# A two-layer hybrid block in split fp32: the opening's loads and root, the key weights' tiles, the conformer's input product, and the second mixer's order are changed

## The chip, the cores and the metric

The kernel runs on one core of one Trainium2 chip. The metric is the device time of one execution in microseconds (us); of the kernel before, three runs were timed. The profile is one further execution, recorded by the hardware profiler. TensorE (PE in the profile) multiplies, VectorE (DVE) and ScalarE (ACT) do elementwise work, GpSimd (POOL) little, and SyncE (SP) issues nearly all DMAs.

## The reference

The block has two layers on 256 tokens `x` and 256 context tokens, 1024 channels wide. Each layer is a half feed-forward, a mixer, and a second half feed-forward; the context goes through all of the first layer, and through the second only as far as the second mixer's keys, values and decays.

```python
x = half_ffn(x, sx[0], sx[1], sx[2], p['ffn1_norm'], p['ffn1_wi'], p['ffn1_wo'])   # and ctx
u_x = modulate(rms_norm(x, p['mix_norm']), sx[3], sx[4]) @ p['w_in']               # and ctx
x = x + sx[5] * mix_tokens(u_x, rows, dirs_x, states_x, p)
x = half_ffn(x, sx[6], sx[7], sx[8], p['ffn2_norm'], p['ffn2_wi'], p['ffn2_wo'])

def conformer_conv(u, dw_w, dw_b, ln_g, ln_b):
    a, g = jnp.split(u, 2, axis=-1)
    h = depthwise_conv(a * jax.nn.sigmoid(g), dw_w, dw_b)
```

`half_ffn` normalises (x times the inverse root of its mean square), scales and shifts by vectors that a product of a conditioning vector with the 1024 by 9216 matrix `ada_w` gives, and applies a gated feed-forward of width 2816. `mix_tokens` joins four mixers: a pooling mixer, a long convolution (hyena), a gated linear attention with decay in chunks of 64 tokens, forward and backward, and the conformer convolution above. All of it is fp32.

## The kernel before, in words

**Products.** Channels lie on partitions, tokens along the free dimension: the 512 tokens of x and context are eight tiles of 128 by 512. An fp32 product is three passes: each operand is split in a high part (a cast on ACT, L172) and a rest (a subtraction on DVE, L173), and `mm3` (L184 to L186) does high by high, high by rest, rest by high. Weights come as raw tiles of up to 1 MB (pool `raw`, 3 buffers) and are split into the pools `whi` and `wlo`, two buffers each; activations and intermediates of 128 by 512 share a pool of 28 buffers (`self.h`), and temporaries one of five. A tile takes a buffer in turn and waits until the last user of that buffer is done.

**Order.** Outside the opening, a planner at compile time sets the order on each engine from program order, priorities (`prio(-PRE)` pulls weight loads, splits and evictions ahead) and its own cost estimates. On the chip each engine takes its instructions in that order.

**Opening** (`start`, its PE, DVE and ACT work in hand-written order). x is loaded as eight tiles of 256 KB, alternating between SP's and ACT's DMA queues (L377); SP then issues the first 2 MB slab of `ada_w` (`ada_fetch`, slab 0), the small vectors and the identity, the first halves of two feed-forward weight tiles, slabs 1 and 2, the second halves, and slab 3. DMAs take eight completion semaphores in turn, and a DMA is issued only when the last user of its semaphore has landed. TensorE first does 48 warm-up products on ones (L152). ACT squares each x tile and DVE adds the squares (L383, L387); `rstd` takes the mean over partitions with 16 small products (L400, L401), and `rsqrt_cols` takes the inverse root on DVE by a shift and three Newton steps, column by column (L211 to L222). Then `part(0)` multiplies slab 0 by the conditioning vector (L287), `keep` does products on ones (L158), `spread` makes diagonal tiles of the root and broadcasts them with TensorE (L232, L234), `ada_end` transposes the row (L299), and DVE and ACT scale and shift x (L425, L432, L433). The products of two 128-row weight tiles follow (L1314 to L1317), interleaved with `part(1)` to `part(3)`.

**Feed-forwards.** 22 weight tiles up, then 8 output tiles down in two halves; between them DVE works off the rest of `ada_w` by multiply-add (L325), two pieces per weight tile.

**Mixer** (`mix`). For keys, values and decay inputs, queries and so on, `group` loads and splits the columns and `fm` (weights stationary) or `tm` (tokens stationary) multiplies. The keys' 128 columns go through `whi` and `wlo` like all others. `conv_in` (step C) loads the convolution's constants, then two groups of 256 columns, gate and value, and does two products of 256 columns for each 128 tokens, followed by tanh (L786) and a multiply (L787). `ORDERS` holds for each layer the program order of the steps: capitals and digits load and multiply a group (`0`, `1`, `2` are hyena's three, `R` gate, `P` pool, `Q` query), small letters advance a generator (`g` decay, states and readout, `h` hyena, `c` convolution, `p` pool, `G` output gate). `g`'s first step is the decay: ACT and DVE work on the product of L1079 up to the scan (L1094).

Of the kernel before, what the change touches and what calls it, by code (L numbers as in the profile page):

```python
# [9 lines left out]
F32 = mybir.dt.float32  # L10
F32R = mybir.dt.float32r
I32 = mybir.dt.int32
U8 = mybir.dt.uint8
AF = mybir.ActivationFunctionType
ALU = mybir.AluOpType
AX = mybir.AxisListType

P = 128
D = 1024
KT = D // P  # L20
# [6 lines left out]
C_K, C_V, C_G, C_Q, C_R, C_POOL, C_HY, C_CONV = 0, 128, 384, 416, 544, 800, 1056, 1824  # L27
# [7 lines left out]
PRE = 400  # L35
# [3 lines left out]
PZ = 2  # L39
F1 = (1.9, 0, 1)  # L40
F2 = (0.8, 0, 1.0, 20)
WARM = 48
KEEP = 2
PIECES = 2
ORDERS = ['Qgg0Rggg1hhghghgPgChcGhGchpchpGch2phpchch', 'Q0g1gggghCh2ghghghccRPhgGchphchchpphhcGpG']
ACTS = [(4, 5, 2, 3, 0, 1, 6, 7), (2, 3, 0, 1, 4, 5, 6, 7)]
TWO_PI_HI = 6.28125
TWO_PI_LO = 2.0 * math.pi - 6.28125
# [3 lines left out]
        ("hy_short_b", 6), ("pool_scale", 2), ("conv_ln_g", 2), ("conv_ln_b", 2), ("conv_dw_b", 2),  # L52
        ("gla_gb_f", 1), ("gla_gb_b", 1), ("gla_norm", 1)]
GROUPS = {"k": [(C_K, 128)], "q": [(C_Q, 128)], "vg": [(C_V, 256), (C_G, 32)], "hy0": [(C_HY, 256)], "hy1": [(C_HY + 256, 256)],
          "hy2": [(C_HY + 512, 256)], "cg": [(C_CONV + 256, 256)], "ca": [(C_CONV, 256)], "r": [(C_R, 256)], "pool": [(C_POOL, 256)]}


class Builder:
# [89 lines left out]
    def warm_up(self):  # L148

        ps = self.pa((P, P))  # L150
        for i in range(WARM):
            self.nc.tensor.matmul(ps, lhsT=self.ones, rhs=self.ones, start=True, stop=True)  # L152
# [35 lines left out]
    def rsqrt(self, src, n, scale):  # L188
        nc = self.nc
        v = self.small(n)  # L190
        nc.vector.tensor_scalar(v, src, scale, EPS, op0=ALU.mult, op1=ALU.add)
        i1 = self.small(n, I32)
        nc.vector.tensor_single_scalar(i1, v.bitcast(I32), 1, op=ALU.logical_shift_right)
        i2 = self.small(n, I32)
        nc.vector.tensor_scalar(i2, i1, -1.0, float(0x5F3759DF), op0=ALU.mult, op1=ALU.add)
        y = i2.bitcast(F32)
        for _ in range(3):
            a = self.small(n)
            nc.vector.scalar_tensor_tensor(a, y, -0.5, y, op0=ALU.mult, op1=ALU.mult)
            b = self.small(n)  # L200
            nc.vector.tensor_tensor(b, a, v, op=ALU.mult)
            y2 = self.small(n)
            nc.vector.scalar_tensor_tensor(y2, b, 1.5, y, op0=ALU.add, op1=ALU.mult)
            y = y2
        return y

# [167 lines left out]
    def load_x(self):  # L374
        self.x = [self.xp.tile([P, 512], F32, tag="x", name=self.nm("x")) for _ in range(KT)]
        for m in range(KT):
            (self.nc.scalar if m % 2 else self.nc.sync).dma_start(out=self.x[m], in_=self.t["xt"][m])  # L377

    def sumsq(self, m, lo, n):

# [8 lines left out]
        else:  # L389
            self.last_sq = sq  # L390

    def rstd(self, lo, n):

        nc = self.nc
        sq = self.last_sq
        nt = n // P
        ps = self.pa((P, nt, 2))
        for j in range(nt):
            a = lo + j * P
            nc.tensor.matmul(ps[:, j, :], lhsT=self.ss[:, a:a + P], rhs=self.mean, start=True, stop=False)  # L400
            nc.tensor.matmul(ps[:, j, :], lhsT=sq[:, j * P:j * P + P], rhs=self.mean, start=False, stop=True)  # L401
        self.r = self.rsqrt_cols(ps, nt)
        return self.r

    def spread(self, lo, r):
# [294 lines left out]
    def mix(self, l, last):  # L700
        nc, t = self.nc, self.t
        T = S if last else 2 * S
        nq = T // S
        w = t["w_in"][l]
        vec = self.vec[l]
        yh, yl = self.norm(l, "mix", 2 * S)
        self.mh, self.ml = {}, {}

        def fm(wg, c, n, TT, lo=0):

            wh, wl = wg
            ps = self.ps((P, TT - lo))
            for k in range(KT):
                self.mm3(ps[:n], wh[:, k, c:c + n], wl[:, k, c:c + n], yh[k][:, lo:TT], yl[k][:, lo:TT], k == 0, k == KT - 1)
            return ps

        sizes = {name: sum(n for _, n in segs) for name, segs in GROUPS.items()}

        def group(name, pieces=1):
            n = sizes[name]  # L720
            at = KT * sum(list(sizes.values())[:list(sizes).index(name)])
            kt = min(KT, 2048 // n)
            with self.prio(-PRE):
                wh, wl = self.whl((P, kt, n))
                raw = self.load(w[:, at:at + kt * n].rearrange("p (k n) -> p k n", k=kt))
                self.split(wh, wl, raw, pieces)
                if kt == KT:
                    return wh, wl
                rest = self.tmp((P, n), name="rest")
                nc.sync.dma_start(out=rest, in_=w[:, at + kt * n:at + KT * n])  # L730
                eh, el = self.h((P, n), F32R, name="rhi"), self.h((P, n), F32R, name="rlo")
                self.split(eh, el, rest)
            return [wh[:, k, :] for k in range(kt)] + [eh], [wl[:, k, :] for k in range(kt)] + [el]

        def tm(wg, tt):

            wh, wl = (a if isinstance(a, list) else [a[:, k, :] for k in range(KT)] for a in wg)
            ps = self.ps((P, wh[0].shape[1]))
            s = slice(tt * P, tt * P + P)
            for k in range(KT):  # L740
                self.mm3(ps, yh[k][:, s], yl[k][:, s], wh[k], wl[k], k == 0, k == KT - 1)
            return ps

        kk, gg, qq = self.h(name="k"), self.h((96, 512), F32R, name="g"), self.h((P, T), name="q")
        wk, wv = group("k"), group("vg", PIECES)
        vv = []
        for v in range(2):
            s = slice(v * S, v * S + S)
            nc.scalar.copy(kk[:, s], fm(wk, 0, P, s.stop, s.start))
            pg = self.pa((96, S))  # L750
            v2 = self.h((P, 2, 256), name="v")
            for j in range(2):
                ps = tm(wv, 2 * v + j)
# [7 lines left out]
        def query():  # L761
            nc.scalar.copy(qq, fm(group("q"), 0, P, T))
# [3 lines left out]
        def conv_in():  # L766

            with self.prio(-PRE):
                kc = cv["k"] = self.rawp.tile([P, CONV_K], F32, tag="raw", name=self.nm("kconv"))
                nc.sync.dma_start(out=kc, in_=t["k_conv"])  # L770
                raw = self.nyp.tile([96, 256], F32, tag="ny", name=self.nm("dwr"))
                dw = cv["dw"] = self.h((96, 256), F32R, name="dw")
                nc.sync.dma_start(out=raw, in_=t["conv_dw"][l])
                self.stack(dw, raw, 1)
                cv["f"], cv["e"] = self.h((96, CONV_K - 1600), F32R, name="cfilt"), self.h((96, T), F32R, name="einv")
                nc.scalar.copy(cv["f"], kc[:96, 1600:CONV_K])
                nc.scalar.copy(cv["e"], kc[:96, 1024:1024 + T])
            wg, wa = group("cg"), group("ca")
            cv["glu"] = []
            for s in range(nq):  # L780
                glu = self.h((P, 2, 256), name="glu")
                for j in range(2):
                    pg, pv = tm(wg, 2 * s + j), tm(wa, 2 * s + j)
                    th = self.tmp((P, 256), name="th")
                    with self.prio(-PRE):
                        nc.scalar.activation(th, pg, AF.Tanh, scale=0.5)  # L786
                        nc.vector.scalar_tensor_tensor(glu[:, j, :], th, 1.0, pv, op0=ALU.add, op1=ALU.mult)  # L787
                cv["glu"].append(glu)

        uc, rr, up = [], [], []  # L790
# [40 lines left out]
        steps = {"0": lambda: hy(0), "1": lambda: hy(1), "2": lambda: hy(2), "Q": query, "C": conv_in, "R": gate_in, "P": pool_in}  # L831
        for step in ORDERS[l]:
            if step in gens:
# [424 lines left out]
    def start(self):  # L1258
# [3 lines left out]
        nc = self.nc  # L1262
# [24 lines left out]
        with self.tc.manual_schedule(engines={et.PE, et.DVE, et.Activation}):  # L1287
            self.ada_init(craw)
            self.warm_up()
            for m in range(KT):  # L1290
                self.sumsq(m, 0, 512)
            r = self.rstd(0, 512)
            yh = [self.yp.tile([P, 512], F32R, tag="y", name=self.nm("yh")) for _ in range(KT)]
            yl = [self.yp.tile([P, 512], F32R, tag="y", name=self.nm("yl")) for _ in range(KT)]
            up = [self.up_tiles(512) for _ in range(2)]
# [23 lines left out]
            def split(i, q):  # L1319
                p = slice(4 * q, 4 * q + 4)  # L1320
                self.split(up[i][0][:, p], up[i][1][:, p], raws[i][:, p])

            def part(q):
                acc = self.pa()
                self.gemv(ws[q], range(KT), acc)
                return self.ada_row(acc)

            def norm(q, row):
                self.ada_end(q, row)
                self.derive(0, [1], two, 2 * q, 2 * q + 2)  # L1330

            def feats(q):
                scale(range(2 * q, 2 * q + 2))
                shift(range(2 * q, 2 * q + 2))

            row = part(0)
            self.keep(KEEP)
            split(0, 0)
            self.spread(0, r)
            norm(0, row)  # L1340
            self.keep(KEEP + 1)
            feats(0)
            split(1, 0)
            mm(0, [0, 1])
# [215 lines left out]
```

## Time and profile before

| | |
|---|---|
| three runs | 1696.96, 1698.08, 1700.32 us (median 1698.08) |
| the profiled execution, its own time | 1701.51 us |
| its span in the profile | 1699.7 us |
| granted TensorE clock, mean | 0.998 |
| busy: PE, PE weight loads, DVE, ACT | 1679.3 (99%), 1440.9 (85%), 1194.5 (70%), 576.7 (34%) us |
| chain that ended last | PE 93%, DVE 3%, DMA 2%, ACT 1%, issue 1% |
| DMA | 262.57 MB, mean 154 GB/s; first of 40 slices 327 GB/s |

The span holds only what the profiler recorded, and the execution is 1.81 us longer. A matmul's busy time overlaps the next one's, since the ends are modelled; how densely TensorE works is read from the distance between two starts. The windows view gives an engine's busy time in a stretch, with the granted clock (1.00 is 2.4 GHz, 0.50 is 1.2 GHz), the mean share of the 16 DMA engines and the bytes per time. The waits view names who waited for whom.

### The profile page before, as it was taken

How to read it: one execution, taken by the hardware profiler on the slowest of the kernel's cores; microseconds unless marked ns; L12 is line 12 of the kernel's file. 1: busy time of each engine (PE TensorE's matmuls, PEld its weight loads, DVE VectorE, ACT ScalarE, POOL GpSimd, SP SyncE). 2: the span in 40 equal slices, each digit the busy share in tenths (PEclk: the TensorE clock that was granted, in tenths of full speed). 3: DMA queues.
4: the chain of work that ended last, by engine and by line, in shares of the span. 5: the costliest groups of instructions: out<-in, count | busy, mean ns of one | idle time of the engine just before them, and what ended most of it. 6: DMA issues, size and time to landing. Idle time of an engine off the chain costs nothing.

```text
span 1699.7 us, 23628 instructions
## 1 busy us (share of the span) xinstructions
PE 1679.3 (99%) x9688; PEld 1440.9 (85%) x9688; DVE 1194.5 (70%) x2085; ACT 576.7 (34%) x741; POOL 33.7 (2%) x59
## 2 busy tenths in 40 slices
PE   9999999999999999999999999999999998999998
PEld 6788888879888898888888898888878897899998
DVE  4899866897675678888669776654464678875455
ACT  3422212333532443222122242221233264554343
POOL 0000000010000000000000000000000000000010
PEclk9999999999999999999999999999999999999999
DMA  8655544533332235545445425444433244345552
GB/s 327 229 182 185 210 153 157 176 128 105 102 108 85 95 127 179 183 163 183 164 149 191 167 102 194 163 156 154 151 124 102 91 133 160 114 152 178 181 196 77
DMA packets 50877, 262.57 MB, mean 154 GB/s; under 512 B 5946, under 2 KB 10880, under 8 KB 28240
## 3 DMA queue, kind: packets, MB, share of 16 engines
q1 hardware_dynamic: 48672, 255.99, 43.0%
q0 software_dynamic: 1376, 4.00, 0.6%
q8 instruction: 76, 1.25, 0.3%
q10 hardware_dynamic: 720, 1.06, 0.2%
q14 instruction: 33, 0.27, 0.0%
HBM read 257.88 MB, written 3.15 MB: 154 GB/s over the span
## 4 chain that ended last, share of the span: by engine, by line
PE 93%; DVE 3%; DMA 2%; ACT 1%; issue 1%; SPq 0%; POOL 0%; DVEq 0%; ACTq 0%; POOLq 0%
PE psm L184 28%; PE psm L185 28%; PE psm L186 28%; DVE acc L325 1%; DVE wlo L173 1%; ACT whi L172 1%; DMA x<-in_xt_dram 1%; PE psa L990 1%; PE psa L1049 0%; PE psm L1314 0%; PE psa L1227 0%; PE psa L234 0%; PE psm L1315 0%; PE psm L1317 0%; PE psa L158 0%
## 5 line engine op out<-in xcount | busy, mean ns | idle before, releaser
L186 PE MATMUL psm<-yh,wlo 128*128 128x512 f32 (+1 forms) x1584 | 557.1, 353 | 2.4 <-DVE wlo L173 2.4
L185 PE MATMUL psm<-yl,whi 128*128 128x512 f32 (+1 forms) x1584 | 558.2, 353 | 0.1
L184 PE MATMUL psm<-yh,whi 128*128 128x512 f32 (+1 forms) x1584 | 556.8, 354 | 1.4 <-DVE glu L787 0.9
L172 ACT CAST whi<-raw 128x2048 fp32r<-128x2048 f32 (+5 forms) x176 | 305.0, 1735 | 598.4 <-PE psm L185 525.9
L173 DVE TENSOR_TENSOR wlo<-raw,whi 128x2048 fp32r<-128x2048 f32 (+5 forms) x176 | 364.6, 2072 | 139.7 <-ACT whi L172 139.4
L186 PEld LDWEIGHTS psm<-yh,wlo 128*128 128x128 f32 x1584 | 299.2, 189 | 44.7 <-DVE wlo L173 3.3
L184 PEld LDWEIGHTS psm<-yh,whi 128*128 128x128 f32 x1584 | 298.0, 189 | 44.6 <-issue 2.3
L185 PEld LDWEIGHTS psm<-yl,whi 128*128 128x128 f32 x1584 | 299.4, 189 | 40.9 <-DVE yl L433 0.5
L325 DVE SCALAR_TENSOR_TENSOR acc<-adaw,cvec,acc 128x512 f32<-128x512 f32 x392 | 274.7, 749 | 2.8
L184 PE MATMUL psm<-hh,whi 128*128 128x512 f32 (+1 forms) x752 | 265.1, 353 | 0.0
L186 PE MATMUL psm<-hh,wlo 128*128 128x512 f32 (+1 forms) x752 | 264.4, 352 | 0.0
L185 PE MATMUL psm<-hl,whi 128*128 128x512 f32 (+1 forms) x752 | 264.3, 351 | 0.0
L186 PEld LDWEIGHTS psm<-hh,wlo 128*128 128x128 f32 x752 | 142.3, 189 | 19.3 <-DVE acc L325 0.8
L185 PEld LDWEIGHTS psm<-hl,whi 128*128 128x128 f32 x752 | 142.3, 189 | 19.3 <-DVE hl L173 0.4
L184 PEld LDWEIGHTS psm<-hh,whi 128*128 128x128 f32 x752 | 142.2, 189 | 18.8 <-issue 0.2
L507 DVE TENSOR_TENSOR sg<-psm,sg 128x512 f32<-128x512 f32 (+1 forms) x90 | 54.4, 607 | 129.5 <-PE psm L186 119.8
L490 DVE SCALAR_TENSOR_TENSOR x<-psm,gt,x 128x256 f32<-128x256 f32 x112 | 50.5, 479 | 115.9 <-PE psm L186 115.8
L506 ACT ACTIVATE sg<-psm 128x512 f32<-128x512 f32 (+1 forms) x90 | 47.9, 533 | 208.9 <-PE psm L186 204.3
L383 ACT ACTIVATE sq<-x 128x512 f32<-128x512 f32 (+1 forms) x64 | 32.7, 522 | 94.8 <-DVE x L490 74.8
L184 PE MATMUL psm<-whi,yh 128*128 128x256 f32 (+1 forms) x200 | 57.3, 291 | 0.0
L186 PE MATMUL psm<-whi,yl 128*128 128x256 f32 (+1 forms) x200 | 57.2, 289 | 0.0
L185 PE MATMUL psm<-wlo,yh 128*128 128x256 f32 (+1 forms) x200 | 57.0, 288 | 0.0
(292 smaller groups left out, 1544.6 us busy)
## 6 DMA issues: line engine op xcount, KB each, us to landing
raw<-in_ffn_wi_dram SPq DMA_DIRECT2D x86, 1024.0 KB, 4.8
adaw<-in_ada_w_dram SPq DMA_DIRECT2D x68, 1024.0 KB, 5.1
raw<-in_ffn_wo_dram SPq DMA_DIRECT2D x32, 896.0 KB, 4.6
raw<-in_ffn_wo_dram SPq DMA_DIRECT2D x16, 1024.0 KB, 5.0
raw<-in_w_in_dram SPq DMA_DIRECT2D x14, 1024.0 KB, 4.8
raw<-in_w_out_dram SPq DMA_DIRECT2D x8, 1024.0 KB, 4.8
adaw<-in_ada_w_dram SPq DMA_DIRECT2D x16, 256.0 KB, 5.5
pm<-in_k_pool_dram SPq DMA_DIRECT2D x12, 256.0 KB, 3.7
```

Of the source, the lines that this page charges most:

```text
L172: self.nc.scalar.copy(hi[:, s], src[:, s])
L173: self.nc.vector.tensor_tensor(lo[:, s], src[:, s], hi[:, s].bitcast(F32), op=ALU.subtract)
L184: mm(ps, lhsT=ah, rhs=bh, start=first, stop=False)
L185: mm(ps, lhsT=ah, rhs=bl, start=False, stop=False)
L186: mm(ps, lhsT=al, rhs=bh, start=False, stop=last)
L325: nc.vector.scalar_tensor_tensor(acc, ws[half][:, k, :], sc, acc, op0=ALU.mult, op1=ALU.add)
L383: nc.scalar.activation(sq, self.x[m][:, lo:lo + n], AF.Square)
L490: nc.vector.scalar_tensor_tensor(self.x[m][:, s], ps[:, v * S - lo:v * S - lo + S], gate[v][:, m:m + 1], self.x[m][:, s], op0=ALU.mult, op ...
L506: nc.scalar.activation(sg, w[2][:, s], AF.Silu)
L507: nc.vector.tensor_tensor(sg, w[3][:, s], sg, op=ALU.mult)
L990: nc.tensor.matmul(ps[par], lhsT=fwd[:, 2 * i + par, :], rhs=cur[par], start=True, stop=True)
```

## The change

x goes over SP's queue alone; 38 warm-up products in place of 48; the first root is `rsqrt_all`, which works on all four columns at once; one `keep` product stands right behind `rstd`'s; `part(0)` is followed by `spread` directly, without the two `keep` products between them, and the split of the first weight quarter stands behind `spread`; two `keep` products in place of three precede the first feature tiles. The key weights are split in two pieces into four tiles of the 28-buffer pool (`keys`) and not into `whi` and `wlo`. The conformer's gate and value columns are one group (`wide`): two loads of four 128-channel blocks by 512 columns, and one product of 512 columns for each 128 tokens. The second layer's order of steps has `g` before `0`, `0` and `1` together, and `C` behind `2` and three generator steps.

```diff
-WARM = 48
+WARM = 38
-ORDERS = [..., 'Q0g1gggghCh2ghghghccRPhgGchphchchpphhcGpG']
+ORDERS = [..., 'Qg01ggggh2hghChgghccRPhgGchphchchpphhcGpG']
-          ... "cg": [(C_CONV + 256, 256)], "ca": [(C_CONV, 256)], ...
+          ... "ca": [(C_CONV + 256, 256), (C_CONV, 256)], ...
+    def rsqrt_all(self, ps, n):
...
+        for _ in range(3):
+            a, y2 = self.small(n), self.small(n)
+            nc.vector.tensor_tensor(a, y, y, op=ALU.mult)
+            nc.vector.tensor_tensor(a, a, vh, op=ALU.mult)
+            nc.vector.scalar_tensor_tensor(y2, a, 1.5, y, op0=ALU.add, op1=ALU.mult)
+            y = y2
+        return y
     def load_x(self):
-            (self.nc.scalar if m % 2 else self.nc.sync).dma_start(out=self.x[m], in_=self.t["xt"][m])
+            self.nc.sync.dma_start(out=self.x[m], in_=self.t["xt"][m])
+        def wide(name):
+            at = KT * sum(list(sizes.values())[:list(sizes).index(name)])
+            his, los = [], []
+            with self.prio(-PRE):
+                for i in range(2):
+                    wh, wl = self.whl((P, KT // 2, 512))
+                    self.split(wh, wl, self.load(w[:, at + 2048 * i:at + 2048 * i + 2048].rearrange("p (k n) -> p k n", k=KT // 2)))
+                    his += [wh[:, k, :] for k in range(KT // 2)]
+                    los += [wl[:, k, :] for k in range(KT // 2)]
+            return his, los
+        def keys():
+            with self.prio(-PRE):
+                raw = self.load(w[:, :KT * P].rearrange("p (k n) -> p k n", k=KT))
+                hi, lo = [], []
+                for i in range(0, KT, 4):
+                    hl = [self.h((P, 4, P), F32R, name) for name in ("khi", "klo")]
+                    self.split(*hl, raw[:, i:i + 4])
+                    for dst, a in zip((hi, lo), hl):
+                        dst += [a[:, k, :] for k in range(4)]
+            return hi, lo
-        wk, wv = group("k"), group("vg", PIECES)
+        wk, wv = keys(), group("vg", PIECES)
-            wg, wa = group("cg"), group("ca")
+            wc = wide("ca")
-                    pg, pv = tm(wg, 2 * s + j), tm(wa, 2 * s + j)
+                    ps = tm(wc, 2 * s + j)
-                        nc.scalar.activation(th, pg, AF.Tanh, scale=0.5)
-                        nc.vector.scalar_tensor_tensor(glu[:, j, :], th, 1.0, pv, op0=ALU.add, op1=ALU.mult)
+                        nc.scalar.activation(th, ps[:, 0:256], AF.Tanh, scale=0.5)
+                        nc.vector.scalar_tensor_tensor(glu[:, j, :], th, 1.0, ps[:, 256:512], op0=ALU.add, op1=ALU.mult)
     def start(self):
-            r = self.rstd(0, 512)
+            r = self.rstd(0, 512, self.rsqrt_all)
+            self.keep(1)
...
             row = part(0)
-            self.keep(KEEP)
+            self.spread(0, r)
             split(0, 0)
-            self.spread(0, r)
             norm(0, row)
-            self.keep(KEEP + 1)
+            self.keep(2)
```

## Rows read from the trace of the kernel before

**Rows 1.** Timeline of PE: start, duration (us), instruction; feed-forward and conformer products.

```profile
337.06 0.39 PE L184 MATMUL psm<-yh,whi 128*128 128x512 f32 x1
...
360.18 0.39 PE L184 MATMUL psm<-yh,whi 128*128 128x512 f32 x1
...
501.12 0.28 PE L186 MATMUL psm<-whi,yl 128*128 128x256 f32 x1
...
502.92 0.28 PE L186 MATMUL psm<-whi,yl 128*128 128x256 f32 x1
```

**Rows 2.** Timeline of the opening, all engines (SPq is SP's DMA issue).

```profile
0.72 1.81 SPq L377 DMA_DIRECT2D x<-in_xt_dram  x4
...
0.98 12.44 PE L152 MATMUL psa<-ones 128*128 128x128 f32 x96 [0.98 <-POOL ones L139]
...
6.87 1.49 DVE L387 SCALAR_TENSOR_TENSOR sq<-sq,sq 128x512 f32<-128x512 f32 x2 [6.87 <-ACT sq L383]
...
15.58 0.63 ACT L383 ACTIVATE sq<-x 128x512 f32<-128x512 f32 x1 [2.09 <-DMA x<-in_xt_dram]
...
18.05 3.42 PE L287 MATMUL psa<-adaw,c 128*32 128x512 f32 x16
18.16 0.16 DVE L211 TENSOR_SCALAR sm<-psa 128x4 int32<-128x4 int32 x1 [3.67 <-PE psa L401]
18.35 0.17 DVE L213 TENSOR_SCALAR sm<-sm 128x4 int32<-128x4 int32 x1
...
21.00 0.36 DVE L222 SCALAR_TENSOR_TENSOR sm<-sm,sm 128x1 f32<-128x1 f32 x4
...
21.40 1.98 PE L158 MATMUL psa<-ones 128*128 128x512 f32 x4
...
23.72 1.13 PE L234 MATMUL psa<-diag,ones 128*128 128x128 f32 x8 [0.34 <-DVE diag L232]
...
25.50 2.82 PE L158 MATMUL psa<-ones 128*128 128x512 f32 x6
...
26.82 1.07 SPq L264 DMA_DIRECT2D adaw<-in_ada_w_dram  x2
...
27.76 0.79 PE L1314 MATMUL psm<-yh,whi 128*128 128x512 f32 x1
...
31.02 1.92 PE L287 MATMUL psa<-adaw,c 128*32 128x512 f32 x16
...
43.87 1.92 PE L287 MATMUL psa<-adaw,c 128*32 128x512 f32 x16
```

**Rows 3.** Windows: stretch, length, busy PE, PEld, DVE, ACT, POOL, clock, DMA share, GB/s.

```profile
2.00:4.00 2.00, 2.00 (x11) 2.00 (x11) 0.00 (x0) 0.00 (x0) 0.41 (x2) 1.00 0.93 314
...
6.00:8.00 2.00, 2.00 (x20) 2.00 (x19) 1.02 (x2) 1.36 (x3) 0.14 (x1) 1.00 1.04 386
...
18.00:20.00 2.00, 2.00 (x13) 0.62 (x17) 1.74 (x15) 0.00 (x0) 0.00 (x0) 0.50 0.89 283
```

**Rows 4.** DMA issues of 27 to 28 us: count, size, us from issue to landing.

```profile
adaw<-in_ada_w_dram SPq DMA_DIRECT2D x2, 1024.0 KB, 11.1
```

**Rows 5.** Waits of PE, whole span: us in total, times, longest.

```profile
PE psa L1112 <- DVE kexp L1108: 2.1, 2, 1.6
...
PE psm L184 <- DVE glu L787: 0.9, 1, 0.9
```

**Rows 6.** Timeline of the second mixer.

```profile
1360.69 2.33 DVE L173 TENSOR_TENSOR wlo<-raw,whi 128x1152 fp32r<-128x1152 f32 x2
...
1380.21 1.44 SPq L1069 DMA_DIRECT2D gwr<-in_gla_gw_dram  x1
...
1397.55 0.70 PE L1079 MATMUL psa<-g,gw 96*128 96x512 f32 x2
...
1409.23 0.66 PE L1112 MATMUL psa<-ident,kexp 128*128 128x128 f32 x4 [1.62 <-DVE kexp L1108]
```

**Rows 7.** Waits of SP's DMA queue, whole span: us in total, times, longest.

```profile
SPq L773 <- DVE yl L433: 24.1, 2, 12.3
```

More of the change, by code (lines that the diff above doesn't have):

```diff
@@ L41 @@
 F2 = (0.8, 0, 1.0, 20)
-WARM = 48
+WARM = 38
 KEEP = 2
 PIECES = 2
-ORDERS = ['Qgg0Rggg1hhghghgPgChcGhGchpchpGch2phpchch', 'Q0g1gggghCh2ghghghccRPhgGchphchchpphhcGpG']
+ORDERS = ['Qgg0Rggg1hhghghgPgChcGhGchpchpGch2phpchch', 'Qg01ggggh2hghChgghccRPhgGchphchchpphhcGpG']
 ACTS = [(4, 5, 2, 3, 0, 1, 6, 7), (2, 3, 0, 1, 4, 5, 6, 7)]
@@ L54 @@
 GROUPS = {"k": [(C_K, 128)], "q": [(C_Q, 128)], "vg": [(C_V, 256), (C_G, 32)], "hy0": [(C_HY, 256)], "hy1": [(C_HY + 256, 256)],
-          "hy2": [(C_HY + 512, 256)], "cg": [(C_CONV + 256, 256)], "ca": [(C_CONV, 256)], "r": [(C_R, 256)], "pool": [(C_POOL, 256)]}
+          "hy2": [(C_HY + 512, 256)], "ca": [(C_CONV + 256, 256), (C_CONV, 256)], "r": [(C_R, 256)], "pool": [(C_POOL, 256)]}
 class Builder:
@@ L203, in rsqrt @@
             nc.vector.scalar_tensor_tensor(y2, b, 1.5, y, op0=ALU.add, op1=ALU.mult)
+            y = y2
+        return y
+    def rsqrt_all(self, ps, n):
+        nc = self.nc
+        i1 = self.small(n, I32)
+        nc.vector.tensor_single_scalar(i1, ps[:, :, 0].bitcast(I32), 1, op=ALU.logical_shift_right)
+        i2 = self.small(n, I32)
+        nc.vector.tensor_scalar(i2, i1, -1.0, float(0x5F3759DF), op0=ALU.mult, op1=ALU.add)
+        y = i2.bitcast(F32)
+        vh = self.small(n)
+        nc.vector.tensor_copy(vh, ps[:, :, 1])
+        for _ in range(3):
[3 more added lines that the diff above has]
+            nc.vector.scalar_tensor_tensor(y2, a, 1.5, y, op0=ALU.add, op1=ALU.mult)
             y = y2
@@ L390, in sumsq, with rstd @@
             self.last_sq = sq
-    def rstd(self, lo, n):
+    def rstd(self, lo, n, root=None):
         nc = self.nc
@@ L401, in rstd @@
             nc.tensor.matmul(ps[:, j, :], lhsT=sq[:, j * P:j * P + P], rhs=self.mean, start=False, stop=True)
-        self.r = self.rsqrt_cols(ps, nt)
+        self.r = (root or self.rsqrt_cols)(ps, nt)
         return self.r
@@ L709, in fm @@
         def fm(wg, c, n, TT, lo=0):
-            wh, wl = wg
+            wh, wl = (a if isinstance(a, list) else [a[:, k, :] for k in range(KT)] for a in wg)
             ps = self.ps((P, TT - lo))
             for k in range(KT):
-                self.mm3(ps[:n], wh[:, k, c:c + n], wl[:, k, c:c + n], yh[k][:, lo:TT], yl[k][:, lo:TT], k == 0, k == KT - 1)
+                self.mm3(ps[:n], wh[k][:, c:c + n], wl[k][:, c:c + n], yh[k][:, lo:TT], yl[k][:, lo:TT], k == 0, k == KT - 1)
             return ps
```

## The prediction, made before the change was run

> **What bounds the kernel now.** I read the page's busy times and chain first (they stand in the table above): PE is busy 99% of the span and carries 93% of the chain, so time is won only by taking work or holes out of TensorE's own sequence. I then read the timeline for the distance between starts, because busy time overlaps. From 337.06 to 360.18 lie 102 products of 512 columns, 0.2267 us each; from 501.12 to 502.92 lie 15 of 256 columns, 0.120 us each [rows 1]. The reader should see that both are dense: a stretch of such products can't be shortened by faster helpers. The holes are in two places. The opening's timeline shows the first product of real work at 27.76 us; before it PE runs warm-ups, the root's small products, the first `ada_w` product, and products on ones [rows 2]. The waits view shows PE held in the mixers by the decay (2.1 us) and by the conformer's multiply (0.9 us) [rows 5].
>
> **The opening, PE's side.** The last x tile reaches ACT at 15.58 [rows 2]. It came over ACT's queue while SP's queue was already moving slab 0. After the change all x stands ahead of slab 0 on one queue. Eight issues at 0.45 us each (1.81 us for four [rows 2]) end at 4.3 us. At the mean of 314 and 386 GB/s [rows 3] the 2.1 MB take 6.0 us, so x is there a little after 8 us. DVE's additions are then the later chain: the first starts at 6.87 as now, six at 0.75 us end at 11.35 [rows 2]. The warm-up loses ten products, that is 20 of its 96 instructions; at 20 per 2 us (6 to 8 us [rows 3]) that is 2.0 us, and it ends at 13.42 - 2.0 = 11.4 us. So `rstd` starts at 11.4. Now, from the last x's square (16.21) to the `ada_w` product (18.05) pass 1.8 us for 14 of the 16 small instructions [rows 2]; with 2.0 us it ends at 13.4.
>
> On DVE the root now takes 18.16 to 21.36, 3.2 us for 27 instructions, of which the first three take some 0.5 us and 24 the rest. The new one has three plus nine, each waiting for the one before. The trace has no such chain of four columns in full; its bounds are 0.11 us (the mean of the 24) and 0.19 us (18.16 to 18.35, where the second waits for the first [rows 2]). I take 0.19: 0.5 + 1.7 = 2.2 us, so the root is there at 15.7. On PE `keep(1)` is two instructions of the 2.82 us for six [rows 2]: 0.9 us, to 14.3. `part(0)` follows at full speed, 1.92 us as at 31.02, in place of 3.42 at 18.05 [rows 2], and ends at 16.2; its slab needs 2.1 MB more behind x, 5 to 6 us at the same rates, so it lands at 13.5 to 14 and doesn't hold. `spread` and `ada_end` took 23.72 to 25.50, 1.8 us, and the first product came 2.26 us after that [rows 2]. `keep(2)` in place of three takes 0.9 us off PE there, but it is covered: scale, cast and shift of the first features take those 2 us too. The two products on ones between `part(0)` and `spread` (1.98 us) go. Sum: 16.2 + 0.3 (eviction) + 1.8 + 2.26 = 20.6 us in place of 27.76: PE gains 7.1 us. What is late next is the identity and the first weight quarter, which come behind slab 0; up to 0.5 us, so 6.6 to 7.1.
>
> **The opening, the stream's side.** PE asks for slab 3 at 43.87 [rows 2]. Its second half was issued at 26.82 + 1.07 - 0.33 = 27.56 and landed 11.1 us later, at 38.7 [rows 2, 4]; PE needs it half-way through its product, at 44.8. That is 6.1 us of slack, less than PE's 7.1. The windows show the DMA engines at a share of 0.89 to 1.04 [rows 3], with the same bytes in nearly the same order after the change, so slab 3 hardly lands earlier. The page "DMA: Bandwidth & Descriptors" of the Trainium skill (section "Issuing engines are not separate DMA queues") says that DMAs of all issuing engines run on the same 16 engines and that several issuers save only issue time. The trace agrees, with shares near 1 while two queues were fed; by that rule the gain is 6.1 us, and without it 7.1.
>
> I take 6.2 us for the opening. Its bounds are 4.5 (the clock, below) and 7.1. Behind it PE is dense, so the shift lasts to the end.
>
> **Conformer product.** Pairs of 256-column products become one of 512: for 4 and 2 token tiles, 8 blocks, 3 passes, (96 + 48) = 144 pairs. Each saves 2 x 0.120 - 0.2267 = 0.013 us [rows 1], 1.9 us in all. Mixer products are often less even; I take 1.7, bounds 0 and 2.5. Loads, bytes and splits stay two of 1 MB per layer. Tanh now starts only when gate and value are done, but the multiply waited for both already, and two PSUM buffers fewer are held for each layer's pair of tiles, so the 0.9 us of [rows 5] should shrink (counted below).
>
> **Key weights.** ACT and DVE split the same bytes in two pieces, two instructions more. What moves is the value weights' split: it gets a `whi` buffer one turn earlier, so the 2.33 us on DVE at 1360.69, in the midst of the norm [rows 6], go ahead of it. PE is dense from there on, so I put this at 0, between a gain of 0.8 (half of one `keep`) and a loss in a rival below.
>
> **Second mixer's order.** `g` before `0` brings the decay's weights forward: their DMA (1380.21) stands behind the convolution's load, which waits for a buffer for up to 12.3 us [rows 6, 7], and step `C` with this load now comes later. The chain from L1079 (1397.55) to the transposes (1409.23) is 11.7 us [rows 6]; PE fills it now with the conformer's products and still waits 1.62. Started earlier, it should hold PE less; the conformer's products come later, when hyena keeps DVE busy. Of the 2.1 + 0.9 us in [rows 5] I take 2.0 as gained. Bounds: 5.5 (all waits of that mixer up to the hyena products, of which the rows show the two largest groups), and a loss of 4.3: if the chain starts no earlier and has only hyena's third group ahead of it, 48 products by 0.120 = 5.8 us [rows 1], 5.9 us stay open in place of 1.6.
>
> **Sum.** 6.2 + 1.7 + 2.0 = 9.9 us: 1691.6 against the profiled execution's own 1701.51. That one is 3.4 us above the median of the runs, so against them it is 1698.1 - 9.9 = 1688.2 us.
>
> **Rivals.**
> *The clock falls again.* At 18 to 20 us the granted clock was 0.50 (1.2 GHz) [rows 3], after PE had stood still for most of the time from 13.4 to 16.3 waiting for x. The new opening still has a thin stretch, the 16 small products and the wait for the diagonals. Then `part(0)` costs 3.42 again and the two later steps some 1 us more: 2.5 us on PE's side, 4.6 in place of 7.1, in all 4.6 + 1.7 + 2.0 = 8.3: 1689.8 us. The page "TensorE: Matmul & The Clock Gate" (section "HAM oscillation — how this bites in real kernels") of the Trainium skill says that idle gaps bring the slow clock back, which speaks for this; that x no longer comes late speaks against.
> *The decay lies open.* The loss of 4.3 above: 6.2 + 1.7 - 4.3 = 3.6, 1694.5 us. For it speaks that nothing but hyena's third group stands between; against, the earlier load.
> *x lands no earlier.* If one queue takes its tiles at a slower pace than two, `rstd` starts at 16.3 as now. The shorter root, the removed `keep` and the shorter way to the first product leave 27.76 - (16.3 + 20.6 - 11.4) = 2.3 us: in all 6.0, 1692.1 us.
> *SP's queue is held (slower).* Four more tiles in the 28-buffer pool bring each mixer's reuse of the long-lived key and query tiles four allocations nearer. If a load of hyena's constants must wait for one, all weight loads behind it on SP wait too. [Rows 7] price one such hold at 12.3 us, 24 in both mixers; one group's products (5.8 us) hide a part: 18.3 - 9.9 = 8.4 us slower, 1706.5. It turns the sign once the holds exceed 9.9 us.
>
> **Chances.** Forecast 0.55, its own range 1684.5 to 1691.5; clock 0.17; open decay 0.14; late x 0.05; held queue 0.05; something unnamed 0.04. Unknown costs at their best give 7.1 + 2.5 + 5.5 = 15.1 (1683.0), at their worst 4.5 + 0 - 4.3 = 0.2 (1697.9). The range is 1683.5 to 1694: it leaves out the held queue, part of the open decay and the far ends. 0.2% is 3.4 us, about what a measurement here can tell from no change. Faster than 1694.7: forecast, clock, late x and most of the open decay, 0.87; within: 0.08; slower: 0.05.
>
> **What would show it.** Right: the last square before 11 us; the first L1314 near 20.6; a clock of 1.00 from 12 to 20 us; the first `ada_w` product in 1.9 us; PE waiting some tenths for slab 3 at about 37.8; L184 to L186 with 512 columns and tokens stationary at 0.23 us; L1079 in the second mixer some 8 us nearer to the mixer's start, and less than 1 us of waits on `kexp`. Wrong: a first L1314 later than 22, PE idle in the first feed-forward, a longer list of waits in the second mixer, or SP waiting for `ke` or `k` with weight loads behind it.

## The result, and the profile after

The changed kernel takes 1688.78 us in the median of four runs (1688.33 to 1689.03), the kernel before 1698.79 (1696.96 to 1700.32, four runs). The ratio is 0.9943, with a 95% interval of 0.9931 to 0.9956: 10.0 us faster, where 9.9 was predicted. Two of these four runs of before (1699.50 and 1700.32 us) are among its longest: 66 more runs of it, made beside the experiments, have medians of 1697.62 to 1697.80 us, and against those the gain is 8.9 us. The profiled execution has a span of 1686.8 us and a mean clock of 0.999.

The page's busy line of after: PE is as full as before, and 6.6 us shorter.

```profile
PE 1672.7 (99%) x9520; PEld 1428.9 (85%) x9520; DVE 1194.1 (71%) x2072; ACT 577.1 (34%) x743; POOL 33.6 (2%) x59
```

Timeline of after's opening (start, duration, instruction; the lines of this kernel stand 18 to 43 lower than those of before, so L305 is the `ada_w` product, L1357 the first feed-forward product):

```profile
0.72 3.73 SPq L395 DMA_DIRECT2D x<-in_xt_dram  x8
0.98 10.38 PE L152 MATMUL psa<-ones 128*128 128x128 f32 x76 [0.98 <-POOL ones L139]
...
5.70 4.05 ACT L401 ACTIVATE sq<-x 128x512 f32<-128x512 f32 x6 [0.74 <-DMA x<-in_xt_dram]
6.36 3.88 DVE L405 SCALAR_TENSOR_TENSOR sq<-sq,sq 128x512 f32<-128x512 f32 x5 [0.68 <-ACT sq L401]
...
11.19 0.28 PE L418 MATMUL psa<-mean,sq 128*128 128x2 f32 x2
...
13.08 0.16 DVE L211 TENSOR_SCALAR sm<-psa 128x4 int32<-128x4 int32 x1 [2.84 <-PE psa L419]
...
13.93 1.92 PE L305 MATMUL psa<-adaw,c 128*32 128x512 f32 x16
...
15.05 0.16 DVE L221 SCALAR_TENSOR_TENSOR sm<-sm,sm 128x4 f32<-128x4 f32 x1
...
19.64 0.50 PE L1357 MATMUL psm<-yh,whi 128*128 128x512 f32 x1
...
22.73 2.38 PE L305 MATMUL psa<-adaw,c 128*32 128x512 f32 x16
...
26.04 1.07 SPq L282 DMA_DIRECT2D adaw<-in_ada_w_dram  x2
...
36.01 2.01 PE L305 MATMUL psa<-adaw,c 128*32 128x512 f32 x16
```

The reader should see here, against [rows 2]: the last square ends at 9.75, the last addition at 10.24, and `rstd` follows the warm-up at once (11.19). The root takes 13.08 to 15.21, 2.13 us. `part(0)` takes 1.92 us, and the first real product starts at 19.64. ACT no longer issues four x loads, and squares its first tile at 3.83 (before 5.70). `part(1)` and `part(3)` are the only ones longer than 1.92 us, by 0.46 and 0.09: PE has caught up with its slabs. The window that answers to [rows 3] shows the clock at 1.00 and 387 GB/s:

```profile
18.00:20.00 2.00, 1.92 (x6) 0.69 (x5) 2.00 (x8) 1.32 (x4) 0.00 (x0) 1.00 1.04 387
```

Timeline of after's second mixer (answers to [rows 6]):

```profile
1367.44 0.38 SPq L1111 DMA_DIRECT2D gwr<-in_gla_gw_dram  x1
...
1381.21 0.73 PE L1121 MATMUL psa<-g,gw 96*128 96x512 f32 x2
...
1394.85 0.40 PE L184 MATMUL psm<-whi,yh 128*128 128x512 f32 x1
...
1398.95 0.39 PE L186 MATMUL psm<-whi,yl 128*128 128x512 f32 x1
...
1400.13 0.50 PE L185 MATMUL psm<-wlo,yh 128*128 128x512 f32 x1 [0.79 <-DVE wlo L173]
...
1405.03 0.66 PE L1154 MATMUL psa<-ident,kexp 128*128 128x128 f32 x4 [0.27 <-DVE kexp L1150]
```

The decay's product stands 16.3 us earlier than before, 8.0 us of which are the order's (the rest is the shift that it inherits), as forecast; the load of its weights (`gwr`) is issued 12.8 us earlier. From 1394.85 to 1398.95 lie 18 wide products of the conformer, 0.228 us each, the pitch of [rows 1]. With more of them behind a wait for a weight split (0.79 us at 1400.13), they fill the time up to the transposes at 1405.03, before which PE waits 0.27 us. The waits view of after has 0.3 us on `kexp` where [rows 5] had 2.1, and no line for the conformer's multiply:

```profile
PE psm L186 <- DVE wlo L173: 1.6, 3, 1.0
...
PE psm L185 <- DVE wlo L173: 0.8, 1, 0.8
...
PE psa L1154 <- DVE kexp L1150: 0.3, 1, 0.3
```

**Where the time went.** I compared the starts of the same PE instructions: the norm's small products at the head of each mixer and behind it. The first column is the shift that has built up at the first mixer's norm, the others what each stretch adds (after minus before, profiled executions):

| | to the first mixer | first mixer | between | second mixer |
|---|---|---|---|---|
| after | -7.77 | -0.56 | -0.01 | -4.57 |

So all of it arises in three places, as predicted, but not in the predicted sizes: 7.8 for 6.2, and 5.1 in the mixers for 3.7. The two profiled spans differ by 12.9 us and the medians by 10.0 or 8.9. The experiments show why.

### The profile page after: what moved, and what is told of

Read it like the earlier page. It is cut to its first block, busy times and chain, and to the rows that moved or that the text cites. A ratio compares the mean times of both kernels' runs of the same rounds, so it can differ in the third digit from the quotient of the medians.

```text
span 1686.8 us, 23277 instructions
## 1 busy us (share of the span) xinstructions
PE 1672.7 (99%) x9520; PEld 1428.9 (85%) x9520; DVE 1194.1 (71%) x2072; ACT 577.1 (34%) x743; POOL 33.6 (2%) x59
## 4 chain that ended last, share of the span: by engine, by line
PE 93%; DVE 4%; ACT 1%; DMA 1%; issue 1%; POOL 0%; DVEq 0%; ACTq 0%; POOLq 0%; SPq 0%
PE psm L184 28%; PE psm L185 28%; PE psm L186 28%; DVE wlo L173 1%; DVE acc L343 1%; ACT whi L172 1%; PE psa L152 1%; DMA pm<-in_k_pool_dram 1%; PE psa L1269 1%; PE psa L305 0%; PE psm L1357 0%; PE psa L1032 0%; PE psa L1091 0%; PE psm L1358 0%; PE psa L252 0%
## 5 line engine op out<-in xcount | busy, mean ns | idle before, releaser
L186 PE MATMUL psm<-yh,wlo 128*128 128x512 f32 (+1 forms) x1552 | 547.8, 354 | 1.6 <-DVE wlo L173 1.6
L185 PE MATMUL psm<-yl,whi 128*128 128x512 f32 (+1 forms) x1552 | 548.7, 354 | 0.1
L184 PE MATMUL psm<-yh,whi 128*128 128x512 f32 (+1 forms) x1552 | 546.6, 355 | 1.1 <-DVE uc L848 0.9
L172 ACT CAST whi<-raw 128x2048 fp32r<-128x2048 f32 (+3 forms) x174 | 302.6, 1742 | 598.3 <-PE psm L185 521.4
L173 DVE TENSOR_TENSOR wlo<-raw,whi 128x2048 fp32r<-128x2048 f32 (+3 forms) x174 | 362.2, 2082 | 138.8 <-ACT whi L172 138.4
L186 PEld LDWEIGHTS psm<-yh,wlo 128*128 128x128 f32 x1552 | 293.1, 189 | 44.0 <-DVE wlo L173 2.8
L184 PEld LDWEIGHTS psm<-yh,whi 128*128 128x128 f32 x1552 | 291.9, 189 | 43.6 <-issue 2.0
L450 ACT ACTIVATE yh<-ny,mods 128x256 fp32r<-128x256 f32 x88 | 40.8, 503 | 40.6 <-DVE ny L443 40.4
L173 DVE TENSOR_TENSOR hl<-sg,hh 128x512 fp32r<-128x512 f32 (+1 forms) x90 | 54.2, 604 | 0.4 <-ACT hh L172 0.4
L172 ACT CAST hh<-sg 128x512 fp32r<-128x512 f32 (+1 forms) x90 | 49.2, 548 | 12.0 <-DVE sg L525 12.0
```

The lines of the kernel that those rows point to most:

```text
L172: self.nc.scalar.copy(hi[:, s], src[:, s])
L173: self.nc.vector.tensor_tensor(lo[:, s], src[:, s], hi[:, s].bitcast(F32), op=ALU.subtract)
L184: mm(ps, lhsT=ah, rhs=bh, start=first, stop=False)
L185: mm(ps, lhsT=ah, rhs=bl, start=False, stop=False)
L186: mm(ps, lhsT=al, rhs=bh, start=False, stop=last)
L450: nc.scalar.activation(yh[k][:, s], a, AF.Identity, bias=sh)
```

## Experiments

All times are medians beside runs of before on the same chip (before: 1697.62, 1697.80 and 1697.68 us in the three groups of runs below). The shift in each stretch is read as above, against the profile of before.

### Each part alone on the kernel before

`o_open`: the opening's edits. `o_wide`: `wide` and its product. `o_order`: one string. `o_keys`: `keys`. Their diffs are the hunks of the change's diff.

> Before plus the opening alone (x on one queue, 38 warm-ups, the root of all columns at once, one keep behind rstd, part(0) followed by spread). My theory, from the two traces: this part is worth 7.8 us and all of it arises before the first feed-forward, since the trace after stands 7.78 us earlier at the end of the opening and still at the first mixer. So 7.8 us faster than before (7.3 to 8.3), first real product near 19.6 us. Rival, the cap of the prediction: slab 3 lands where it did and the part gives 6.1 us, the rest of what the trace after shows coming from the other parts.

> Before plus the conformer's gate and value as one product of 512 columns alone. My theory: 144 pairs of products by 0.013 us, of which mixer 1 (96 pairs) gives 0.5 to 1.3 us and mixer 2 (48 pairs) 0.6 us: 1.1 to 1.9 us faster. Rival: the larger gain in the second mixer (4.6 us between the traces) is the wide product's too, through its weight tiles and the multiply that PE waited for: 3 us or more.

> Before plus the second layer's new order of steps alone. My theory: the order is what took 4 us out of the second mixer: 3 to 4.5 us faster, with the wait on kexp under 0.5 us. Rival: the order gains only together with the key tiles or the wide product, since with two groups of gate and value the conformer's loads still take two turns of the weight tiles late: under 1 us, or slower.

> Before plus the key weights in four tiles of the 28-buffer pool alone. My theory: same time within 0.5 us, PE being dense at each mixer's start. Rival: the value weights' split, a turn earlier, takes a hole out at the second mixer's start, or lets the decay start earlier: 1 us faster or more. Other rival: the four tiles bring the reuse of long-lived tiles nearer and SP's queue is held: 1 us slower or more.

| | us | ratio, 95% interval | to the first mixer | first mixer | second mixer |
|---|---|---|---|---|---|
| o_open | 1694.41 | 0.9981 [0.9972, 0.9989] | -7.95 | -0.02 | -0.87 |
| o_wide | 1702.13 | 1.0025 [1.0015, 1.0036] | -3.07 | -0.58 | +5.15 |
| o_order | 1699.10 | 1.0008 [1.0000, 1.0017] | -2.80 | -0.02 | +0.68 |
| o_keys | 1697.21 | 0.9997 [0.9988, 1.0006] | -3.24 | -0.14 | -0.02 |

Only the expectation for the keys held; for the order its rival did. `o_open` missed its expectation (7.8 us) and its rival (6.1), and `o_wide` is slower where both of its theories had it faster. By medians the parts alone give -3.2, +4.5, +1.5 and -0.4: together 2.4 us slower, where all at once are 10 us faster.

**The opening before was a bad one in the profile.** Three of these kernels have the old opening unchanged, and yet their first column says 2.8 to 3.2 us less than the profile of before. The same instructions of `o_keys`, timeline and window:

```profile
0.98 13.80 PE L152 MATMUL psa<-ones 128*128 128x128 f32 x96 [0.98 <-POOL ones L139]
...
11.73 0.63 ACT L383 ACTIVATE sq<-x 128x512 f32<-128x512 f32 x1 [2.02 <-DMA x<-in_xt_dram]
...
16.39 1.92 PE L287 MATMUL psa<-adaw,c 128*32 128x512 f32 x16
...
24.68 0.79 PE L1326 MATMUL psm<-yh,whi 128*128 128x512 f32 x1
```

```profile
18.00:20.00 2.00, 2.00 (x8) 0.68 (x4) 1.97 (x17) 1.10 (x2) 0.00 (x0) 1.00 1.05 391
```

The last square starts at 11.73 (before 15.58), ahead of the warm-up's end; the clock is 1.00 at 18 to 20 us (before 0.50), the DMA moves 391 GB/s (before 283), and the first real product starts at 24.68 (before 27.76). `o_wide` has it at 24.81, `o_order` at 25.24. So some 3 us of what the profiled execution was above the median lay in its opening. Against the three other openings (-3.04 in the mean) the seven profiled executions with the whole new opening (-7.49 in the mean, -6.79 to -7.95) gain 4.5 us, not 7.8. The median of `o_open` gains 3.2; its runs spread from 1692.65 to 1696.64, and what lies behind the spread isn't seen in its one profile. (That profile gains another 0.9 us in the second mixer and loses 1.1 us at the very end, where SP takes 2.93 us to issue the last four output transfers and in after 1.82.) So the opening is worth 3.2 to 4.5 us.

**The wide product alone loses 5.1 us in the second mixer.** Timeline of `o_wide`, PE and DVE, and two windows:

```profile
1415.64 0.43 PE L1162 MATMUL psa<-v,kdt 64*32 64x64 f32 x24
...
1419.15 1.22 PE L1162 MATMUL psa<-v,kdt 64*32 64x64 f32 x24 [2.42 <-DVE st L1168]
...
1451.17 1.01 PE L1187 MATMUL psa<-blk,osq 128*128 128x2 f32 x4 [2.75 <-ACT osq L1185]
```

```profile
1416.02 0.23 DVE L1166 COPY st<-psa 128x64 f32<-128x64 f32 x1 [0.57 <-PE psa L1162]
1416.28 2.29 DVE L173 TENSOR_TENSOR wlo<-raw,whi 128x2048 fp32r<-128x2048 f32 x1
...
1418.82 1.05 DVE L1168 SCALAR_TENSOR_TENSOR st<-st,dec,psa 128x64 f32<-128x64 f32 x3
```

```profile
1415.00:1420.00 5.00, 2.29 (x64) 1.41 (x68) 4.15 (x8) 1.45 (x3) 0.53 (x1) 0.69 1.01 352
1420.00:1425.00 5.00, 5.00 (x28) 4.37 (x29) 2.46 (x9) 3.31 (x10) 0.53 (x1) 0.63 0.56 218
```

The states go to and fro: products of `v,kdt` on PE, a copy and sums (`st`) on DVE, the next products. In `o_wide` the planner put a weight split of 2.29 us on DVE between the copy and the sums, and left no products for PE beside it. PE is busy 2.29 of 5 us, and the clock is at 0.69 and 0.63 in the two windows. At the readout (1451.17) PE stands still for 2.75 us more, and the clock falls again. In the kernel before, the split stands behind the sums, in DVE's timeline:

```profile
1423.88 2.29 DVE L173 TENSOR_TENSOR wlo<-raw,whi 128x2048 fp32r<-128x2048 f32 x1 [1.30 <-ACT whi L172]
```

### Undoing one part of the kernel after

```diff
# u_wide: two groups, two products again (the group table, tanh and multiply go back with them)
-            wc = wide("ca")
+            wg, wa = group("cg"), group("ca")
-                    ps = tm(wc, 2 * s + j)
+                    pg, pv = tm(wg, 2 * s + j), tm(wa, 2 * s + j)
# u_keys
-        wk, wv = keys(), group("vg", PIECES)
+        wk, wv = group("k"), group("vg", PIECES)
# the second layer's order: u_order, u_gfirst, u_clate
-'Qg01ggggh2hghChgghccRPhg...'
+'Q0g1gggghCh2ghghghccRPhg...'
+'Qg01gggghCh2ghghghccRPhg...'
+'Q0g1ggggh2hghChgghccRPhg...'
```

> After with gate and value as two groups and two products of 256 columns again; opening, keys and the second layer's new order kept. My theory: the new order gives nothing without the wide product (alone it lost 0.7 us in the second mixer, and the wide product alone lost 5.1 us there, where the clock fell twice to 0.50); only both together took out 4.6 us. So undoing one loses the whole: 5 to 6 us slower than after, about 1694.5. Rival, the sum of the prediction: the product is worth its 1.7 us alone, 1690.5.

> After with the second layer's old order of steps; opening, keys and wide product kept. My theory: the wide product in the old order opens the hole seen with the wide product alone, PE waits for the state sums and the squared readout and the clock falls to 0.50: 8 to 10 us slower than after, about 1698, mean clock 0.996. Rival: that hole belonged to the key weights' place in the whi and wlo buffers, and with the keys out of them the old order costs the 2 us of the prediction: 1691.

> After with the key weights through whi and wlo again; opening, wide product and order kept. My theory: within 0.7 us of after, as the keys alone changed before by 0.4 us. Rival: what takes 4.6 us out of the second mixer is all three together, the keys' free turn of the weight buffers among them: 2 us slower than after or more.

> After with only the first half of the new order: g before 0 and 1, but the conformer's step C at its old place before 2. My theory: the wide product's place decides, since it keeps the weight buffers and the constants' buffer for longer: 4 us slower than after or more, with PE's long wait between the state products back. Rival: the decay's early start decides and C's place is worth nothing: within 1 us of after.

> After with only the second half of the new order: C late, behind 2 and three generator steps, but hyena's 0 before g as of old. My theory: C's late place keeps conformer products for the time in which the state sums run on DVE, so PE keeps its filler and the clock stays at 1.00; but the decay starts 8 us later and its chain lies open: about as late as with the first half alone, 2 to 4 us slower than after. Rival: the decay's early start is what counts, and without it the whole 9.5 us of the old order come back.

| | us | ratio, 95% interval | first mixer | second mixer |
|---|---|---|---|---|
| u_keys | 1688.96 | 0.9946 [0.9933, 0.9960] | -0.58 | -4.68 |
| u_gfirst | 1691.07 | 0.9959 [0.9947, 0.9971] | -0.58 | -2.15 |
| u_clate | 1694.08 | 0.9976 [0.9967, 0.9985] | -0.69 | +0.74 |
| u_wide | 1695.15 | 0.9984 [0.9976, 0.9993] | -0.13 | +0.77 |
| u_order | 1698.28 | 0.9999 [0.9991, 1.0008] | -0.48 | +4.77 |

The keys are worth nothing, as expected. `u_order` came as expected too (9.5 us slower than after), and `u_wide` lost 6.4 us where I gave 5 to 6. Product and order are one edit with two halves: in the second mixer the wide product costs 4.8 to 5.2 us in the old order, the new order costs 0.7 to 0.8 with the narrow products, and both together gain 4.6 to 4.7. The rival that adds them up (`u_wide` 1690.5, `u_order` 1691) is out.

How much of this is idle time, the windows view tells: the second mixer from the norm's products at its head to those behind it, in before, after, `u_wide` and `o_wide`.

```profile
1353.01:1491.89 138.88, 130.68 (x1123) 119.50 (x1122) 110.53 (x265) 72.60 (x131) 1.05 (x2) 1.00 0.38 129
1344.67:1478.97 134.30, 129.60 (x1075) 116.23 (x1074) 108.32 (x263) 70.90 (x129) 1.72 (x4) 1.00 0.37 129
1346.01:1485.65 139.64, 131.80 (x1122) 120.11 (x1121) 108.48 (x263) 70.88 (x129) 1.72 (x4) 1.00 0.35 123
1349.34:1493.36 144.02, 133.83 (x1074) 120.08 (x1073) 111.07 (x265) 73.00 (x131) 1.05 (x2) 0.95 0.36 125
```

PE stands still for 8.2, 4.7, 7.8 and 10.2 us. So 3.5 of after's 4.6 us are idle time, and 0.6 are the shorter products (48 pairs by 0.0133). In `o_wide` only 2.0 of the 5.1 us lost are idle time: PE is also busy for 3.1 us longer, with shorter products, and this is the one of the four stretches whose clock is below 1.00 (0.95).

Why the order needs the product is in the waits of `u_wide` (`o_order` has the same three):

```profile
PE psm L186 <- DVE wlo L173: 3.0, 4, 1.0
PE psm L185 <- DVE wlo L173: 2.1, 1, 2.1
PE psa L1154 <- DVE kexp L1150: 1.5, 1, 1.5
```

After has 1.6, 0.8 and 0.3 there, 3.9 us less in all (against them stand new, shorter waits, so that the idle time of the mixer falls by 3.1). In the new order the conformer's weights are split while DVE works on the decay. With two groups, PE waits 2.1 us for a split in the midst of them, and then 1.5 us for the decay all the same; with the wide product, whose two weight tiles hold half the channels each, 0.8 and 0.3. That it is the shape of the tiles, and not merely where the planner puts the splits, no run has told apart.

Why the product needs the order is in after's DVE timeline. A split stands in the midst of the states here too:

```profile
1405.99 0.23 DVE L1196 COPY st<-psa 128x64 f32<-128x64 f32 x1
1406.33 1.06 DVE L1198 SCALAR_TENSOR_TENSOR st<-st,dec,psa 128x64 f32<-128x64 f32 x3
1407.31 2.28 DVE L173 TENSOR_TENSOR wlo<-raw,whi 128x2048 fp32r<-128x2048 f32 x1
...
1409.85 0.22 DVE L1196 COPY st<-psa 128x64 f32<-128x64 f32 x1
```

But with `C` late the conformer's products are still there: twelve of 512 columns run from 1405.97 to 1410.02 between and behind after's state products, and PE waits for nothing. The first and the last of them in PE's timeline:

```profile
1405.97 0.50 PE L184 MATMUL psm<-whi,yh 128*128 128x512 f32 x1
...
1409.63 0.39 PE L186 MATMUL psm<-whi,yl 128*128 128x512 f32 x1
```

Of the order's two halves (with the wide product) neither stands for the whole: from +4.8, `g` first gives 6.9 us, `C` late 4.0, both 9.3. My expectations missed both: I gave `u_gfirst` 4 us or more, and it lost 2.3; I gave `u_clate` 2 to 4 us and thought that `C` late alone keeps the filler (the products that PE can do meanwhile) and the clock, and it lost 5.3. Timeline of `u_clate`, DVE and PE, and a window:

```profile
1412.59 2.29 DVE L173 TENSOR_TENSOR wlo<-raw,whi 128x2048 fp32r<-128x2048 f32 x1 [0.51 <-ACT whi L172]
1414.80 0.27 DVE L1198 SCALAR_TENSOR_TENSOR st<-st,dec,psa 128x64 f32<-128x64 f32 x1
```

```profile
1415.22 0.43 PE L1192 MATMUL psa<-v,kdt 64*32 64x64 f32 x8 [2.77 <-DVE st L1196]
```

```profile
1410.00:1415.00 5.00, 1.53 (x27) 0.60 (x25) 4.26 (x8) 1.90 (x1) 0.17 (x1) 0.73 0.62 208
```

With the decay 8.2 us later the last four conformer products run beside the first states and are gone at 1410.6; a split between the sums opens the hole again. The clock does not fall behind this hole but as it begins: the hole starts at 1412.45, and the window from 1412 to 1413 us already has 0.67. Ahead of it lie waits of 0.93 and 0.76 us and short products, and no run tells which of these counts. In `u_gfirst`, where the products are gone too, the planner put that split behind the sums, PE has no such hole, and most of the loss of 2.3 us is a wait of 1.8 us for a split.

### What the opening hangs on

```diff
# u_queue
-            self.nc.sync.dma_start(out=self.x[m], in_=self.t["xt"][m])
+            (self.nc.scalar if m % 2 else self.nc.sync).dma_start(out=self.x[m], in_=self.t["xt"][m])
# u_warm30
-WARM = 38
+WARM = 30
# u_root
-            r = self.rstd(0, 512, self.rsqrt_all)
+            r = self.rstd(0, 512)
```

> After with x alternating over SP's and ACT's queues again, all else kept. My theory: x on one queue is the larger half of the opening's gain. With two queues the odd tiles share the engines with slab 0, the last square comes at 14 to 16 us in place of 9.2 us, PE waits for it with only 76 warm-up products ahead, and the first real product comes at 23 to 25 us: 3 to 4 us slower than after. Rival: the stream sets the opening's end, slab 3 lands at the same time, and it costs 1 us or less.

> After with 30 warm-up products in place of 38. My theory: after the change the stream bounds the opening (part(1) waited 0.46 us for its slab and part(3) 0.1 us), so an earlier start of PE buys nothing: the first real product up to 0.9 us earlier, but the products behind part(3) at the same time, same time as after within 0.4 us. Rival: PE bounds it, and the 0.9 us that the sums of squares leave go through to the end: 0.9 us faster. Second rival: the shorter warm-up lets the clock fall in more executions, 1 us slower.

> After with the first root column by column again (27 short instructions in place of 12). My theory: the root takes 3.2 in place of 2.1 us, so the diagonals come 1.1 us later and with them the first real product, but the waits that PE has for the slabs take 0.5 us of it back: 0.4 to 0.9 us slower than after, more where the hole lets the clock fall. Rival: the root lies beside part(0) and costs nothing.

| | us | ratio, 95% interval | first real product | to the first mixer |
|---|---|---|---|---|
| u_queue | 1689.03 | 0.9951 [0.9937, 0.9964] | 21.03 | -7.30 |
| u_warm30 | 1689.03 | 0.9950 [0.9938, 0.9963] | 20.35 | -7.30 |
| u_root | 1689.70 | 0.9954 [0.9942, 0.9967] | 21.52 | -6.59 |

`u_queue` was my largest miss: 3 to 4 us expected, 0.2 measured. Its ACT and PE timeline:

```profile
12.02 0.63 ACT L401 ACTIVATE sq<-x 128x512 f32<-128x512 f32 x1 [1.88 <-DMA x<-in_xt_dram]
```

```profile
36.93 1.92 PE L305 MATMUL psa<-adaw,c 128*32 128x512 f32 x16
```

The last square over two queues starts anywhere from 11.73 to 15.58 in five executions (over one queue all squares have ended at 9.75 to 10.78 in nine), and here at 12.02; in this execution `rstd` waited little for it, and slab 3 held nothing. Over one queue x comes earlier and more evenly, but none of the five runs of `u_queue` (1688.67 to 1690.31) shows that this saves time.

`u_warm30` shows the new bound. PE's timeline:

```profile
11.07 0.35 PE L418 MATMUL psa<-mean,sq 128*128 128x2 f32 x2 [1.40 <-DVE sq L405]
...
37.82 1.07 PE L305 MATMUL psa<-adaw,c 128*32 128x512 f32 x8 [0.46 <-DMA adaw<-in_ada_w_dram]
```

With eight warm-ups fewer PE waits 1.40 us for the squares and then 0.46 us for slab 3, and the time is that of after within 0.4 us, as expected: nothing is left to win there. The root by columns costs 0.7 us beside the two others of its group and 0.9 beside after, the upper end of what I gave, and the wait for the diagonals is seen in its row:

```profile
17.70 1.13 PE L252 MATMUL psa<-diag,ones 128*128 128x128 f32 x8 [0.77 <-DVE diag L250]
```

So none of these three costs more than 0.9 of the 3.2 to 4.5 us. No run goes back to 48 warm-ups or puts the two `keep` products back behind `part(0)`, and the rest lies there as far as the rows tell: from `o_keys` to `o_open` the warm-up's end comes 2.6 us earlier (14.78 to 12.16), and the way from there to the first real product is 1.6 us shorter (9.9 to 8.3).

## Why the prediction came out, point by point

**The sum was right, its terms were not.** The opening gives 3.2 to 4.5 us (predicted 6.2), product, order and keys together 5.1 (predicted 3.7). An opening that was 1.7 to 3 us too large and mixers that were 1.4 too small nearly cancelled, and the rest of the match is luck: of the 10.0 us, 1.1 come from the four runs of before that after was measured against.

**The step that failed in the opening** is the last one of the sum: 9.9 us were worked out against an execution of 1701.51 and then taken off a median that is 3.4 us lower. I wrote that difference down and didn't ask which rows held it. They were in front of the reader, in the opening: 3.42 us for 16 products at 18.05 that take 1.92 at 31.02 [rows 2], with a clock of 0.50 and 283 GB/s [rows 3]. An edit that removes a mishap of the profiled execution removes nothing from executions that don't have it. The cap of 6.1 us has the same fault. The second half of slab 3 lands at 36.92 to 39.14 us in the fourteen profiled executions, whichever the opening (before 38.70, after 36.92; issue plus the time to landing), so it hardly lands earlier, as I wrote. But PE asks for it at 44.8 us only in the profile of before; in `o_keys`, `o_order` and `o_wide` it asks at 41.7 to 42.3. Their slack is 2.7 to 4.6 us, which is about what the opening gives. Against the profile of before the term was too small (7.8), since in after the slab also landed 1.8 us earlier. That the stream would be late next was right; it holds PE for 0.09 us in after and 0.46 in `u_warm30`.

**Steps that held:** the root's 2.2 us (2.13), `part(0)` at 1.92, 0.228 us per wide product, 0 for the keys. The first product at 20.6 (19.64 to 20.75 in the six undisturbed executions) held in part by luck: the warm-up ends at 11.36 us in after, as predicted, but at 12.1 to 12.5 in the five others, and the way from there took 8.3 us and not 9.2, as `rstd` and the steps behind `part(0)` were each some 0.5 us shorter. The rule of the page "DMA: Bandwidth & Descriptors" of the Trainium skill, section "Issuing engines are not separate DMA queues", was used for the cap; `u_queue` agrees with it, as the second issuing queue changes the time by 0.2 us. What was wrong in the cap was the execution that I read it from.

**The rival "the clock falls again"** (0.17) is real but cheap: one of seven profiled executions of the new opening has it (`u_wide`: `part(0)` takes 3.24 us, and the first column has -6.88, where the others have -6.79 to -7.95). It costs little since slab 3 lands there at 38.08, and PE, whose first product comes 2 us behind after's, asks for the second half at 38.4. Waiting didn't bring it: PE stands still for less than 0.1 us from the warm-up's end to this fall; what came before are the 16 small products of `rstd`, two on ones and the start of `part(0)`. Where I hadn't looked for it, in the second mixer, it weighs more, around the holes of 2.4 to 2.8 us of `o_wide`, `u_order` and `u_clate`.

**Product and order.** 1.7 us by 144 pairs were right per product, and in the first mixer 0.56 us of 1.28 (96 x 0.0133) came through; there the conformer's products got 1.2 us shorter by their starts, and much of it went back as longer distances between the Fourier and inverse products (0.5 and 0.4 us, the same in `o_wide`). Why these distances grew stays open. In the second mixer the term has no meaning by itself, since its sign hangs on the order. The order's 2.0 us were worked out from waits on `kexp` and the multiply, which both went as told; the term was mis-sized since I priced each edit against the kernel before. What came nearest to a rival is "the decay lies open": `u_clate` and `u_order` show such a hole, but a few products later, at the state sums, and not where the edits stand together. Neither the late x nor the held queue showed.

## What to carry to other kernels

Before a sum is made against a profiled execution, look where it differs from the median: here the rows at half clock and the low DMA rate were that execution's own, and the edit that removed them was worth less in the median. When products get shorter or move, ask which chain they cover: a planner places them and the weight splits anew, and here a split of 2.3 us inside a chain between two engines cost the wait and the slow clock around it. Edits that move the same filler (an order and a product's shape) have to be priced together.

## What was not expected of the hardware

The moment at which TensorE first runs at its full pace differs between executions. (The windows view shows 1.00 there from the start, in [rows 3] too; the pace has to be counted.) In the profile of before, windows of 1 us count 7 warm-up products from 3 to 4 us and 11 from 4 to 5; in `o_keys` they count 7 still from 6 to 7 and 11 from 7 to 8. With it moves the end of the same 96 warm-up instructions: 13.42 us in the profile of before, 14.78 in `o_keys`. The one with the earlier end is the one that then waited for x, had the clock fall, and lost 3 us. A late x alone didn't do it: `o_order`, with the end at 14.02, waits 1.16 us for x in the midst of `rstd`, and its clock stays at 1.00.

The mean clock of a run tells of large falls without a trace: all eleven runs of `u_order` show 0.996 and all four of after 0.999 or 1.000. For single small falls it is a weak sign: of 30 runs of before the 14 with 1.000 take 1696.56 to 1697.70, the six with 0.998 1697.39 to 1699.71, but the ten with 0.999 1696.97 to 1700.34, the longest of all among them.
